# Attention over short sequences: three input buffers, a TensorE loop of twelve steps, and more stores among the loads

## Chip, cores, metric

The kernel runs on one core of one Trainium2 chip. The metric is device time in microseconds (us), lower is better. Times of one kernel on one chip spread by 1 to 3% (the kernel before, 23 runs on one chip: 135.31 to 139.74 us); the state of a run (fast or slow) is given by rule, a run more than 1.5% above the fastest of its kernel counting as slow.

## The reference

For each of 32 x 12 heads, a sequence of 128 and a head dimension of 64, all float32:

```
scores = (1 / sqrt(64)) * q @ k.T
attn   = softmax(scores, axis=-1)
out    = attn @ v
```

This is 37.75 MB to read and 12.58 MB to write for little arithmetic.

## The kernel before

The heads are cut into 48 units of 8 heads. Four units form a group, and a group needs one load each of q, k and v (1 MB read, 0.5 MB written, the tensors being float32 and the buffers bfloat16: the page has 37.75 MB read from HBM for 36 loads and 512.0 KB for each of them). A unit becomes one or two stores. All loads and most stores are issued by GpSimd (POOL) in one program order. TensorE (PE) runs a real loop of `PERIOD` steps. One step holds transposes (T), a reordering of v (V), scores (S) and attention times v (O, Q), each of another unit: T runs five steps ahead of O.

```python
PERIOD, FIRST = 8, -8                        # loop of 8 steps; the first is step -8
TRIPS = NU // PERIOD + 1                     # NU = 48 units
NQ, NVB, NVE, NT, NA = 2, 2, 8, 2, 4         # buffers of q and k, v, reordered v, transposes, attn
MIXED, OWN, HELD = 28, 40, NU - 8            # units stored among the loads
...
# a load waits until its buffer was read by TensorE
if x >= NVB: deps = [("V", sum(vgroups[:x - NVB + 1]) - 1)]                    # v
if x >= NQ:  deps = [("T", t) for t in t_order if t[0] == x - NQ and t[1] == j] # q, k
...
# after the k load of group x: the stores that are due
while kind == "k" and sum(stores[:todo[0] + 1]) <= MIXED * (x - 4) / (len(supers) - 5):
    store(todo.pop(0))
```

The first real work is at step -5, so in the first trip the steps before it have nothing to do, and in the last trip some pieces have nothing to do. Each piece of the loop is therefore under a test of the trip number. Neighbouring pieces that are skipped in the same trip share one test, that is one jump over all of them:

```python
for place in [(l, kind) for l in range(PERIOD) for kind in "TVSOQ"]:
    ...
    skipped = 0 if trips[0] else TRIPS - 1
    if waiting or not places or places[-1][0] != skipped or place == (2, "T"):
        places.append((skipped, waits[place] if waiting else [], []))
    places[-1][2].append((ops[place], [] if waiting else waits[place]))
...
with nc.Fori(0, TRIPS, ..., head_slot={nc.tensor.engine: 144}):   # place of the loop's first
    for skipped, always, some in places:                          # instruction in a block, taken
        run_waits("PE", always)                                   # as 256 from the stops below
        with nc.tensor.If_ne(trip, skipped):
            for o, w in some:
                run("PE", o, w)
    nc.tensor.reg_add(trip, trip, 1)
```

The softmax here doesn't subtract the row's maximum and nothing guards it: scores larger than these inputs give would overflow.

Of the kernel before, what the change touches and what calls it, by code (L numbers as in the profile page):

```python
# [10 lines left out]
def kernel(  # L11
# [7 lines left out]
    nc = tc.nc  # L19
# [12 lines left out]
    NU = B * H // 8  # L32
# [31 lines left out]



    PERIOD, FIRST = 8, -8
    TRIPS = NU // PERIOD + 1


# [7 lines left out]
        v_at[m - 4] = [m]  # L78
    steps = range(min(t_at), NU + 1)

    NQ, NVB, NVE, NT, NA = 2, 2, 8, 2, 4



    MIXED, OWN, HELD = 28, 40, NU - 8

    HALVES = NU - 5

# [360 lines left out]
    def waits_of(engine, o):  # L449
        out = []  # L450
        for name, value in needed(engine, o, c).items():
            have = seen[engine].get(name, 0)
            if value > have:
                out.append((name, value - have if engine == "PE" else value))
                seen[engine][name] = value
        return out

    def run_waits(engine, waits):
        for name, value in waits:
            i = ENGINE[engine].wait_ge(sems[name], value)  # L460
            if engine == "PE":
                i.then_inc(sems[name], -value)
# [3 lines left out]
    def run(engine, o, waits):  # L466
        e = ENGINE[engine]
        run_waits(engine, waits)
        for s, value in o.dma:
            e.wait_ge(s, value)  # L470
        if o.emit is None:

            untold[engine] = o.marks
            return
        i = o.emit()
        for n, name in enumerate(o.marks):
            (i if n == 0 else e.drain()).then_inc(sems[name], 1 + untold[engine].count(name))  # L477
        untold[engine] = []

    def tensor_program():  # L480

        ops, waits, when = {}, {}, {}
        for o in program["PE"]:
            trip, l = divmod(at_step[o.key] - FIRST, PERIOD)
            place = l, o.key[0]
            w = waits_of("PE", o)
            assert waits.setdefault(place, w) == w and not o.dma, (o.key, w, waits[place])
            when.setdefault(place, []).append((trip, o.emit is None))
            if trip == 2:
                ops[place] = o  # L490
        places = []
        for place in [(l, kind) for l in range(PERIOD) for kind in "TVSOQ"]:
            trips = [t for t, empty in when[place] if not empty]
            assert trips in (list(range(TRIPS - 1)), list(range(1, TRIPS))), (place, trips)
            waiting = len(when[place]) > len(trips)
            assert not waiting or len(when[place]) == TRIPS
            skipped = 0 if trips[0] else TRIPS - 1
            if waiting or not places or places[-1][0] != skipped or place == (2, "T"):
                places.append((skipped, waits[place] if waiting else [], []))
            places[-1][2].append((ops[place], [] if waiting else waits[place]))  # L500
        trip = ctx.enter_context(nc.tensor.register("trip"))
        nc.tensor.reg_mov(trip, 0)


        with nc.Fori(
                0, TRIPS, engines=bass.OrderedEngineSet([nc.tensor.engine]),
                head_slot={nc.tensor.engine: 144}):
            for skipped, always, some in places:
                run_waits("PE", always)
                with nc.tensor.If_ne(trip, skipped):  # L510
# [3 lines that stand above are left out]
# [11 lines left out]
    nc.gpsimd.drain()  # L525

    tensor_program()


# [51 lines left out]
```

## Time and profile before

| | before |
|---|---|
| time, median of 3 runs | 136.31 us (135.97 to 136.35) |
| span of the profiled run | 133.8 us |
| busiest compute engine | PE, 70% of the span |
| DMA, mean over the span | 236 GB/s on the written side |
| instruction fetches of TensorE (queue q8) | 4 of 16,384 bytes, at 2.6, 8.3, 15.2 and 20.8 us |

In the rows of 40 slices each slice is a fortieth of that run's span (3.3 us here); digits are busy tenths. In a row of a timeline the first number is the start, the second the busy time, "x16" a count of merged instructions, and the bracket tells how long the engine had stood idle and what ended that. The landing times quoted below come from the trace's completion records: a transfer is counted as landed when the last of the 16 DMA engines that report on it has done so. Fetch times come from its transfer records. That q8 serves TensorE is an inference.

### The profile page before, as it was taken

The page shows a single profiled execution, that of the slowest core. Times are in us where ns is not written, and L with a number is a line of the kernel's source. Part 1 is how long each engine was busy: PE and PEld are TensorE (multiplying, and loading weights), DVE is VectorE, ACT ScalarE, POOL GpSimd, SP SyncE. Part 2 cuts the span into 40 slices and gives each one's busy share as a digit, 9 for nine tenths or more (in the row PEclk, how much of TensorE's full clock was granted, in tenths as well). Part 3 has the DMA queues.
Part 4 walks back from the last instruction along what each step waited for, and adds up shares of the span by engine and source line. Part 5 has one row for each costly group of instructions (what it writes and reads, how often), then busy time and mean ns, then how long its engine had stood idle before and what let it go on. Part 6 is the DMA issues. An engine that isn't in the chain of part 4 may idle for free. (4 is left out here: it accounts for less than half of the span.)

```text
span 133.8 us, 6648 instructions
## 1 busy us (share of the span) xinstructions
PE 93.1 (70%) x2880; PEld 63.3 (47%) x2880; DVE 75.0 (56%) x164; ACT 73.8 (55%) x97; POOL 57.5 (43%) x81
## 2 busy tenths in 40 slices
PE   0052788969869898588657897667897696595820
PEld 0040545636546665365435565445565464464510
DVE  1020346858768775656647458548457547485850
ACT  0005157686758886275573565582656654768700
POOL 5902024060510957705903924914913999500000
PEclk9999999999999999779997579998569869999555
DMA  2999999999999999999999999999999999999971
GB/s 13 162 200 210 200 211 180 194 199 172 212 200 210 188 163 241 309 200 263 314 198 257 319 202 248 327 200 245 331 201 241 331 205 235 390 403 389 359 243 68
DMA packets 24392, 31.56 MB, mean 236 GB/s; under 512 B 1344, under 2 KB 15680, under 8 KB 24384
## 3 DMA queue, kind: packets, MB, share of 16 engines
q0 software_dynamic: 22208, 29.36, 106.7%
q1 hardware_dynamic: 2176, 2.10, 4.6%
q8 instruction: 4, 0.07, 0.2%
q14 instruction: 4, 0.03, 0.1%
HBM read 37.75 MB, written 12.58 MB: 376 GB/s over the span
## 5 line engine op out<-in xcount | busy, mean ns | idle before, releaser
L241 DVE COPY qkT<-qk_ps 128x1024 bf16<-128x1024 bf16 x48 | 33.1, 689 | 34.3 <-DMA k_b<-in_k_dram 19.4
L224 ACT CAST v_e<-v_ps 128x512 bf16<-128x512 f32 x48 | 28.3, 590 | 41.6 <-PE v_ps L186 26.6
L229 ACT ACTIVATE attnT<-s_ps 128x1024 bf16<-128x1024 f32 x48 | 49.5, 1032 | 1.1 <-PE s_ps L205 1.1
L254 DVE TENSOR_TENSOR o_sb<-o_ps,recip 128x512 f32<-128x512 f32 (+1 forms) x53 | 34.0, 642 | 4.8
L383 POOL DMA_DIRECT2D v_b<-in_v_dram x12 | 10.8, 901 | 52.7 <-PE v_ps L186 47.1
L176 PE MATMUL qk_ps<-ident,q_b 128*64 128x128 bf16 x384 | 17.0, 236 | 17.5 <-PEq L460 17.3
L368 POOL DMA_DIRECT2D out_dram<-o_sb x38 | 27.7, 733 | 0.6 <-DVEq L477 0.6
L176 PE MATMUL qk_ps<-ident,k_b 128*64 128x128 bf16 x384 | 18.9, 253 | 12.4 <-PEq L460 12.3
L216 PE MATMUL o_ps<-v_e,attnT 128*32 128x65 bf16 x1536 | 24.1, 205 | 2.2 <-PEq L460 2.0
L176 PEld LDWEIGHTS qk_ps<-ident,q_b 128*64 128x64 bf16 x384 | 13.4, 119 | 20.3 <-issue 19.9
L186 PE MATMUL v_ps<-v_b,sel 128*32 128x512 bf16 x192 | 21.1, 430 | 2.4 <-PEq L460 1.4
L176 PEld LDWEIGHTS qk_ps<-ident,k_b 128*64 128x64 bf16 x384 | 15.2, 131 | 15.5 <-issue 14.5
L216 PEld LDWEIGHTS o_ps<-v_e,attnT 128*32 128x32 bf16 x1536 | 17.8, 101 | 8.7 <-issue 5.2
L205 PE MATMUL s_ps<-qkT 64*128 64x128 bf16 x384 | 20.8, 233 | 0.8 <-PEq L460 0.6
L205 PEld LDWEIGHTS s_ps<-qkT 64*128 64x128 bf16 x384 | 11.8, 100 | 12.7 <-issue 12.7
L251 DVE RECIPROCAL recip<-o_ps 128x8 f32<-128x8 f32 (+1 forms) x53 | 10.5, 199 | 11.8 <-PE o_ps L216 11.3
L395 POOL DMA_DIRECT2D q_b<-in_q_dram x12 | 8.8, 737 | 5.2 <-PE qk_ps L176 4.1
L186 PEld LDWEIGHTS v_ps<-v_b,sel 128*32 128x32 bf16 x192 | 5.1, 94 | 7.9 <-issue 4.7
L395 POOL DMA_DIRECT2D k_b<-in_k_dram x12 | 8.5, 707 | 0.0
L224 ACT ACT_TABLE_LOAD x1 | 1.3, 1283 | 10.8 <-DMA v_b<-in_v_dram 10.8
L539 DVE COPY sel<-ident 128x128 bf16<-128x128 bf16 x1 | 0.2, 227 | 2.2 <-POOL ident L519 2.2
L365 POOL DMA_DIRECT2D out_dram<-o_sb x2 | 1.5, 742 | 0.0
(7 smaller groups left out, 1.1 us busy)
## 6 DMA issues: line engine op xcount, KB each, us to landing
out_dram<-o_sb POOLq DMA_DIRECT2D x40, 256.0 KB, 11.1
q_b<-in_q_dram POOLq DMA_DIRECT2D x12, 512.0 KB, 12.3
v_b<-in_v_dram POOLq DMA_DIRECT2D x12, 512.0 KB, 10.2
k_b<-in_k_dram POOLq DMA_DIRECT2D x12, 512.0 KB, 11.8
out_dram<-o_sb SPq DMA_DIRECT2D x8, 256.0 KB, 5.4
```

The costliest lines, as they stand in the source:

```text
L176: i = nc.tensor.transpose(p[a * D:(a + 1) * D, :, r4, jj, :], x[:, r, a], ident[:])
L186: x = nc.tensor.matmul(t[r4 * 32:(r4 + 1) * 32], lhsT=sel[:, w, :], rhs=v_b[g % NVB][:, :, r4 * D:(r4 + 1) * D], start=True, stop=True)
L205: i = nc.tensor.matmul(t[:, a, h, :], lhsT=x[p, 1, 4 * w + h, :], rhs=x[p, 0, 4 * w + h, :], start=True, stop=True)
L216: y = nc.tensor.matmul(t[h * SO:(h + 1) * SO, a, r * (D + 1):(r + 1) * (D + 1)], lhsT=x[:, a, h, r * SO:(r + 1) * SO], rhs=v_e[m % NVE][:, ...
L224: return nc.scalar.copy(v_e[m % NVE][:, :, :D], v_ps[:].rearrange("p (n e) -> p n e", e=D))
L229: return nc.scalar.activation(out=attnT[u % NA][:].rearrange("p a h (r s j) -> p (a h r) s j", r=4, j=J), in_=s_ps[u % 2][:].rearrange("p ...
L241: return nc.vector.tensor_copy(x.rearrange("p h (r j s) -> p (h r) j s", r=4, j=J)[:, :, 2 * b:2 * b + 2, :].rearrange("p x j s -> p x (j ...
L251: nc.vector.reciprocal(r, o4[:, :, :, D]).then_inc(s_r, 1)
L254: return nc.vector.tensor_mul(o[:, :, w, :].rearrange("p a (r d) -> p a r d", d=D), o4[:, :, :, :D], r.unsqueeze(3).to_broadcast([128, o4. ...
L368: e.dma_start(out=dst[:, a], in_=src[:, a]).then_inc(s_o[lane(c)], 16)
L383: op("POOL", ("load", kind, x), lambda: nc.gpsimd.dma_start(out=v_b[x % NVB][:], in_=v_rows[:, 2 * first:2 * (first + n), :],).then_inc(s_ ...
L395: nc.gpsimd.dma_start(out=bufs[x % NQ][:], in_=rows[R][:, n:n + 2, :]).then_inc(sm[x % NQ], 16)
```

## The change

The intent is to keep a third group of loads in flight, so that the DMA queue does not run thin, and to store more units among the loads. Three buffers repeat every three groups, that is every twelve steps, so the loop must cover twelve steps. The whole diff:

```diff
-    PERIOD, FIRST = 8, -8
+    PERIOD, FIRST = 12, -12
...
-    NQ, NVB, NVE, NT, NA = 2, 2, 8, 2, 4
-    MIXED, OWN, HELD = 28, 40, NU - 8
+    NQ, NVB, NVE, NT, NA = 3, 3, 12, 3, 4
+    MIXED, OWN, HELD = 32, 40, NU - 8
...
-            if waiting or not places or places[-1][0] != skipped or place == (2, "T"):
+            if waiting or not places or places[-1][0] != skipped:
...
-                head_slot={nc.tensor.engine: 144}):
+                head_slot={nc.tensor.engine: 160}):
```

## The prediction

> **What bounds the kernel now.** I read the page first, then throughput by stretch, then GpSimd's timeline (it issues every load), then the end on VectorE and SP. The page's second part:

> ```profile
> DMA  2999999999999999999999999999999999999971
> GB/s 13 162 200 210 200 211 180 194 199 172 212 200 210 188 163 241 309 200 263 314 198 257 319 202 248 327 200 245 331 201 241 331 205 235 390 403 389 359 243 68
> ```

> The DMA row is full from the second slice to the last but two, while no compute engine is above 70% busy on the page: the transfers are the bound. A busy digit does not say that the transfers run at full rate; the GB/s row does. It counts bytes on the written side, and a load writes half of what it reads (float32 becomes bfloat16), so about 205 for loads and about 400 for stores are the same HBM rate. In this light the 180, 172 and 188, 163 are holes. The next view is busy time, clock, DMA share and GB/s in chosen stretches:

> ```profile
> 10.00:21.00 11.00, 7.01 (x132) 4.08 (x131) 2.94 (x5) 5.11 (x8) 2.51 (x4) 1.00 1.21 209
> 21.30:24.00 2.70, 2.33 (x80) 1.75 (x80) 2.10 (x6) 1.98 (x3) 0.21 (x1) 1.00 1.21 162
> ...
> 29.80:32.60 2.80, 2.40 (x80) 1.75 (x80) 2.20 (x6) 1.41 (x2) 0.00 (x0) 1.00 1.21 164
> 32.60:45.40 12.80, 10.98 (x402) 7.58 (x400) 9.42 (x20) 9.69 (x15) 4.20 (x6) 1.00 1.22 207
> 45.40:51.20 5.80, 5.14 (x200) 3.57 (x191) 5.00 (x10) 4.02 (x6) 3.60 (x6) 1.00 1.22 159
> 61.69:102.48 40.79, 31.68 (x970) 21.57 (x972) 24.36 (x49) 24.16 (x32) 20.98 (x29) 0.83 1.19 258
> 114.00:124.00 10.00, 6.93 (x262) 4.62 (x256) 6.34 (x15) 7.73 (x11) 1.68 (x3) 0.96 1.03 394
> 124.00:132.00 8.00, 3.47 (x116) 2.30 (x112) 4.34 (x16) 2.32 (x3) 0.00 (x0) 0.50 0.79 271
> ```

> See the last column: 207 to 209 where loads are well fed, 162, 164 and 159 in three holes, 394 in the stores after the loads, and 271 in the last 8 us. GpSimd's timeline names the cause of the holes:

> ```profile
> 19.21 0.89 POOL L383 DMA_DIRECT2D v_b<-in_v_dram  x1 [7.85 <-PE v_ps L186]
> ...
> 26.62 0.89 POOL L383 DMA_DIRECT2D v_b<-in_v_dram  x1 [5.11 <-PE v_ps L186]
> ...
> 43.51 0.89 POOL L383 DMA_DIRECT2D v_b<-in_v_dram  x1 [6.15 <-PE v_ps L186]
> ```

> GpSimd stands 5 to 8 us before each v load until TensorE has read the v buffer two groups back; the k load and next q load queue behind it in program order. Each of these three issues is followed, 2 to 3 us later, by a hole. The completion records say the same: v loads land 2.6 us after the transfer before them when fed, but 3.51, 3.36 and 3.59 us after it in the three holes, and the k load after the last one 2.99 instead of 2.5. From 55 us on stores lie between the groups, the queue is deeper at each v issue, and v loads land at 2.65 us again: there the two buffers suffice.

> The end is a second, different limit:

> ```profile
> 116.03 0.69 DVE L241 COPY qkT<-qk_ps 128x1024 bf16<-128x1024 bf16 x1 [1.55 <-DMA k_b<-in_k_dram]
> ...
> 128.82 0.42 DVE L254 TENSOR_TENSOR o_sb<-o_ps,recip 128x256 f32<-128x256 f32 x1
> ```

> The last k load lands at 115.9. VectorE is waiting for it, and the seven steps that remain finish at 129.24; SP issues the last store at 129.32 and it lands at 132.29. So 13.4 us of dependent compute plus about 3 us of store follow the last load. The queue drains in parallel, but 271 GB/s in the last 8 us says it is no longer full: compute hands out the last stores.

> [...] a load group alone costs 3 x 524 KB at 207 GB/s = 7.6 us, a stored unit 262 KB at about 400 = 0.65 us, and a group with four units measures 40.79 / 4 = 10.2 us, equal to 7.6 + 4 x 0.65. Moving a store among the loads hides nothing. [...] in the last store: its first engine reports 1.97 us after issue. [...] The page of before shows four 16 KB instruction fetches (q8, 0.07 MB).

> **The change part by part.**

> Third q, k and v buffer. A v load now waits for the group three back, so one more whole group (7.6 us) is queued when it is issued. That is far above the roughly 1 us by which before falls short, so the holes vanish. Their worth from throughput: 2.70 x (1 - 162/207) + 2.80 x (1 - 164/207) + 5.80 x (1 - 159/207) = 0.59 + 0.58 + 1.34 = 2.5 us. From the landings: 0.9 + 0.75 + 0.95 + 0.5 = 3.1 us. I take **2.8 us** earlier for everything after 55 us.

> The third transposed buffer and the twelve v_e buffers remove waits on VectorE and ScalarE that the trace does not show as costs; TensorE's order of steps is unchanged. Worth 0. They are needed because the loop repeats buffer names every three groups, hence twelve steps.

> Stores among the loads. The condition counts units allowed after k load x as 28(x-4)/7, now 32(x-4)/7, cut to whole stores. Before the last k load (x = 11) GpSimd has queued 24 units; now 4, 8, 12, 18, 22, 26. The last k load therefore stands behind two more units: 2 x 0.65 = **1.3 us later**. In exchange 22 rather than 24 units remain after it. Total bytes do not change. I checked that no store should block a load for long: after k loads 8, 9 and 10 the newest stored unit is finished within a step of the k load's own release, with more than a group still queued.

> Loop of twelve steps. Per unit 60 matmuls and 60 weight loads, so 12 x 120 = 1,440 instructions[...]; six fetches instead of four, once. Trip 0 now skips seven steps instead of three while TensorE waits for the first load (its first matmul is at 7.33 us). Any delay there is covered by nine loads in flight. Worth 0, at worst some tenths.

> Sum. Last k load lands at 115.9 - 2.8 + 1.3 = 114.4. Compute path: + 13.4 = 127.8 for the last store's issue, + 2.2 to 3.0 = 130.0 to 130.8 against 132.3, a gain of 1.5 to 2.3. Drain path: 2.8 less work-time lost, 129.5, not the later one. So the extra early stores give back part of what the buffers win. I choose a gain of 2.1 us: 136.3 - 2.1 = **134.2 us**.

> **Rivals.** (a) The drain sets the end and the compute path has slack: then all 2.8 to 3.1 us arrive, 133.2 to 133.5, just over 2% faster. For it: stores on SP land every 0.65 us up to the last, so the slowest DMA engine still had work. Against it: 271 GB/s in the last 8 us. (b) A new wait: GpSimd, with stores closer behind compute, stalls on an unfinished unit and loads fall behind; or [...] issue slows. For it: GpSimd's single program order. Against: a spare group in the queue. It would give 135 to 136. (c) Holes are not starvation but the v loads' 512-byte packets: no gain, only the 1.3 us later, 137.0 to 137.5. Against it: later v loads land at 2.65 us. (d) TensorE's first trip stalls on fetching the longer loop: some us of early compute, caught up before the end. No cost.

> **Range and chances.** Between (a) and the main sum lie 133.2 and 134.8; the range adds a partial (b) and the run spread of 0.4 us: 133.0 to 135.8. The 2% line is 133.58, inside (a): I give faster 0.31, same 0.67, slower 0.02.

> **What would show it.** No stretch below 195 GB/s between 10 and 50 us; GpSimd's v loads issued at least a group earlier; first stores about 2.5 us earlier in the drain; last k landing near 114.4; still 13 us from there to the last normalise; six fetches on q8. I am wrong if holes persist at the same rate, if the last k load lands before 113.5 or after 116, or if the tail after it shortens by over 1 us (the clock there is 0.50, and a livelier clock could do that).

## More of the kernel before

The page's line on instruction fetches:

```profile
q8 instruction: 4, 0.07, 0.2%
```

It gives the count, the megabytes and the share of the DMA engines' time.

## The result

The changed kernel took **146.97 us** (median of 4 runs, 145.13 to 147.5) against 136.33 us. The ratio is 1.0745, with a 95% interval of 1.0616 to 1.0873: slower by 7%. (A ratio here is the mean time of one kernel's fast runs over that of the other's fast runs of the same rounds, so not quite the ratio of the medians.) The prediction was 134.2 us, and wrong.

The page of the changed kernel (slices of 3.6 us), the rows that answer to those of before, and the line of the instruction fetches:

```profile
DMA  2999999999995099949999999999999999999952
GB/s 14 180 206 206 208 207 202 215 199 210 190 212 100 5 129 162 348 95 141 153 347 194 245 320 199 282 348 200 246 319 196 281 282 202 318 401 394 323 177 79
...
q8 instruction: 11, 0.18, 0.5%
```

From the third slice up to slice 12 the throughput is nearly what was predicted: 190 to 215 with hardly a hole. Then it falls to 100, 5 and 129, and again to 95, 141 and 153, where before had 210, 188, 163. After 73 us the row is again like that of before. So nearly everything is lost between 43 and 73 us. The landing times agree: two v loads land 9.60 and 5.39 us after the transfer before them (2.65 when fed), an excess of 6.95 + 2.74 = 9.7 us, and the last store lands 11.2 us later than before (143.45 against 132.29). The predicted two additional stores ahead of the last k load account for up to 1.3 of that.

What starved the DMA is on GpSimd's timeline:

```profile
19.98 0.89 POOL L383 DMA_DIRECT2D v_b<-in_v_dram  x1 [8.76 <-PE v_ps L186]
...
34.35 0.90 POOL L383 DMA_DIRECT2D v_b<-in_v_dram  x1 [12.07 <-PE v_ps L186]
...
49.50 0.89 POOL L383 DMA_DIRECT2D v_b<-in_v_dram  x1 [12.41 <-PE v_ps L186]
...
63.82 0.90 POOL L383 DMA_DIRECT2D v_b<-in_v_dram  x1 [9.10 <-PE v_ps L186]
```

The v loads come 14 to 15 us apart, while a group of loads lasts 7.6 us. GpSimd waits for TensorE to free a buffer. The buffers are not too few; TensorE is slow. TensorE's timeline in that stretch says why:

```profile
22.21 0.46 PE L216 MATMUL o_ps<-v_e,attnT 128*32 128x65 bf16 x17
25.27 0.41 PE L216 MATMUL o_ps<-v_e,attnT 128*32 128x65 bf16 x15 [2.61 <-issue]
25.61 1.06 PE L176 MATMUL qk_ps<-ident,k_b 128*64 128x128 bf16 x16
...
30.34 0.46 PE L216 MATMUL o_ps<-v_e,attnT 128*32 128x65 bf16 x20
32.86 0.28 PE L216 MATMUL o_ps<-v_e,attnT 128*32 128x65 bf16 x12 [2.06 <-issue]
...
37.08 0.52 PE L216 MATMUL o_ps<-v_e,attnT 128*32 128x65 bf16 x23
40.02 0.27 PE L216 MATMUL o_ps<-v_e,attnT 128*32 128x65 bf16 x9 [2.42 <-issue]
...
44.40 0.40 PE L216 MATMUL o_ps<-v_e,attnT 128*32 128x65 bf16 x26
47.34 0.24 PE L216 MATMUL o_ps<-v_e,attnT 128*32 128x65 bf16 x6 [2.54 <-issue]
```

```profile
PE o_ps L216 <- issue: 15.3, 6, 5.5
```

For much of this stretch TensorE is also slow: 16 transposes often take 1.06 us instead of 0.64, and a step up to 2.65 us instead of 1.7. Why is not shown; the granted clock was 0.93 from 22 to 36 us and 0.74 from 36 to 50 us. From one stop to the next, two steps or half a group, 6.8 to 8.1 us pass, which is the 14 to 15 us per group.

The one piece of the diff that I had not read as a change is the removed `place == (2, "T")`. It broke the long jump of the first trip in two. From the ruler the loop's layout is estimated (head at slot 160, six instructions, then 125 a step): in the changed kernel the first trip's jump over seven empty steps leads from block 0 to about slot 160 + 6 + 7 x 125 = 1041, in block 4, over blocks 1, 2 and 3. Before, with three empty steps and the break, it went from block 0 to block 1 (slot 400) and then to block 2 (slot 525).

### The profile page after: what moved, and what is told of

The parts are those of the page before. It is cut to its first block, busy times and chain, and to the rows that moved or that the text cites. A ratio compares the mean times of both kernels' runs of the same rounds, so it can differ in the third digit from the quotient of the medians.

```text
span 145.0 us, 6636 instructions
## 1 busy us (share of the span) xinstructions
PE 99.2 (68%) x2880; PEld 66.7 (46%) x2880; DVE 75.5 (52%) x168; ACT 74.6 (51%) x97; POOL 57.4 (40%) x81
## 2 busy tenths in 40 slices
DMA packets 24399, 31.68 MB, mean 218 GB/s; under 512 B 1344, under 2 KB 15680, under 8 KB 24384
## 5 line engine op out<-in xcount | busy, mean ns | idle before, releaser
L241 DVE COPY qkT<-qk_ps 128x1024 bf16<-128x1024 bf16 x48 | 33.0, 687 | 23.0 <-PE qk_ps L176 11.0
L216 PE MATMUL o_ps<-v_e,attnT 128*32 128x65 bf16 x1536 | 25.7, 209 | 16.6 <-issue 15.3
L254 DVE TENSOR_TENSOR o_sb<-o_ps,recip 128x512 f32<-128x512 f32 (+1 forms) x53 | 34.0, 642 | 4.8
L383 POOL DMA_DIRECT2D v_b<-in_v_dram x12 | 10.9, 907 | 55.8 <-PE v_ps L186 47.7
L176 PE MATMUL qk_ps<-ident,q_b 128*64 128x128 bf16 x384 | 21.2, 274 | 16.2 <-PEq L460 15.8
L216 PEld LDWEIGHTS o_ps<-v_e,attnT 128*32 128x32 bf16 x1536 | 18.3, 104 | 24.2 <-issue 21.0
L251 DVE RECIPROCAL recip<-o_ps 128x8 f32<-128x8 f32 (+1 forms) x53 | 10.6, 201 | 34.0 <-PE o_ps L216 33.1
L176 PEld LDWEIGHTS qk_ps<-ident,q_b 128*64 128x64 bf16 x384 | 16.8, 144 | 19.1 <-issue 18.3
L186 PE MATMUL v_ps<-v_b,sel 128*32 128x512 bf16 x192 | 22.6, 460 | 1.8 <-PEq L460 1.0
L205 PE MATMUL s_ps<-qkT 64*128 64x128 bf16 x384 | 22.2, 245 | 0.7 <-PEq L460 0.6
L176 PE MATMUL qk_ps<-ident,k_b 128*64 128x128 bf16 x384 | 17.8, 243 | 4.9 <-PEq L460 4.1
L205 PEld LDWEIGHTS s_ps<-qkT 64*128 64x128 bf16 x384 | 12.6, 104 | 14.0 <-issue 14.0
L176 PEld LDWEIGHTS qk_ps<-ident,k_b 128*64 128x64 bf16 x384 | 14.0, 124 | 7.8 <-issue 6.7
L186 PEld LDWEIGHTS v_ps<-v_b,sel 128*32 128x32 bf16 x192 | 5.1, 95 | 7.6 <-issue 4.7
```

Of the source, the lines that this page charges most:

```text
L176: i = nc.tensor.transpose(p[a * D:(a + 1) * D, :, r4, jj, :], x[:, r, a], ident[:])
L186: x = nc.tensor.matmul(t[r4 * 32:(r4 + 1) * 32], lhsT=sel[:, w, :], rhs=v_b[g % NVB][:, :, r4 * D:(r4 + 1) * D], start=True, stop=True)
L205: i = nc.tensor.matmul(t[:, a, h, :], lhsT=x[p, 1, 4 * w + h, :], rhs=x[p, 0, 4 * w + h, :], start=True, stop=True)
L216: y = nc.tensor.matmul(t[h * SO:(h + 1) * SO, a, r * (D + 1):(r + 1) * (D + 1)], lhsT=x[:, a, h, r * SO:(r + 1) * SO], rhs=v_e[m % NVE][:, ...
L241: return nc.vector.tensor_copy(x.rearrange("p h (r j s) -> p (h r) j s", r=4, j=J)[:, :, 2 * b:2 * b + 2, :].rearrange("p x j s -> p x (j ...
L251: nc.vector.reciprocal(r, o4[:, :, :, D]).then_inc(s_r, 1)
```

## The experiments

**Theory "skipped blocks"**: the long jump leaves blocks of the loop unfetched, and the next pass has to fetch block after block on demand, behind the queued loads. **Rivals**: the 32 units among the loads hold up GpSimd ("stores behind compute"); nine loads in flight slow the issue or the transfers ("queue depth"); a loop of seven blocks is too long by itself ("loop too long").

### First set: repair it, or undo one part

**e1_split.** Two breaks, so that the first trip's jumps are short:

```diff
-            if waiting or not places or places[-1][0] != skipped:
+            if waiting or not places or places[-1][0] != skipped or place in ((2, "T"), (4, "T")):
```

> The changed kernel, but TensorE's first trip passes the seven empty steps in three short jumps (about 240 instructions each) instead of one of about 840, so that it touches each 256-instruction block. Theory 'skipped blocks' (the one long jump leaves two blocks of the loop unfetched, and the next pass fetches block after block on demand): TensorE's 2 to 5.5 us stalls between 22 and 62 us vanish, about 7 instruction fetches instead of 11, time 133 to 136 us. Theories 'stores behind compute', 'queue depth' and 'a loop of seven blocks is too long': no change, 145 to 148 us.

Measured: 135.21 us median of 20 runs (133.62 to 136.51) against 136.97; ratio 0.9839 (0.9801 to 0.9876), 1.6% faster than before. Six fetches. One condition in the building of the loop is worth 9% of the time. All three rivals fall: stores, buffers and the loop's length are those of the slow kernel. Two stops, of 2.88 and 1.98 us, remain; they end at 19.3 and 24.8 us. The first matmul is at 12.9 us instead of 7.2.

**e2_first5.** `FIRST = -5`: the first trip has work in each step, and no jump passes a block.

```diff
-    PERIOD, FIRST = 12, -12
+    PERIOD, FIRST = 12, -5
```

> The changed kernel with the loop's first step at -5 instead of -12: the first trip has work in every step and jumps over single pieces only. The loop has the same length. 'Skipped blocks': no long stalls, 6 or 7 fetches, 133 to 136 us. 'Loop too long': fetch stalls remain at the same places of the loop, 143 us or more. 'Stores' and 'queue depth': unchanged, 145 to 148 us.

Measured: 139.83 us against 136.97, ratio 1.0231 (1.0126 to 1.0335), and six fetches. Of the ten surplus us about three are left: fetches at 32.3 and 39.9 us come with stops of 4.48 and 1.93 us. So the theory is too narrow. In this run blocks that are reached for the first time late, when nine loads stand in the queue and TensorE has work, go with these stops even though nothing was skipped; to that extent the rival "loop too long" has a share. (The profiled run was slow; the stops are read for their presence only.)

**e3_mixed28.** 28 units among the loads as before.

```diff
-    MIXED, OWN, HELD = 32, 40, NU - 8
+    MIXED, OWN, HELD = 28, 40, NU - 8
```

> The changed kernel with 28 units among the loads as before. 'Stores behind compute': the loss goes, 135 to 137 us. 'Skipped blocks' and the others: the stalls are in TensorE before most stores, so 144.5 to 147 us, at most 1.3 us better.

Measured: 145.89 us, ratio 1.0683 (1.0589 to 1.0778), eleven fetches (the profiled run was a slow one). The stores are not the cause.

**e4_depth2.** Three buffers, but loads wait for the group two back.

```diff
-            if x >= NVB:
-                deps = [("V", sum(vgroups[:x - NVB + 1]) - 1)]
+            if x >= 2:
+                deps = [("V", sum(vgroups[:x - 1]) - 1)]
...
-        if x >= NQ:
-            deps = [("T", t) for t in t_order if t[0] == x - NQ and t[1] == j]
+        if x >= 2:
+            deps = [("T", t) for t in t_order if t[0] == x - 2 and t[1] == j]
```

> The changed kernel with three buffers, but each load still waits for the group two back, so no more loads are in flight than before. 'Queue depth' (nine loads in flight slow the issue or the transfers): back to 136 to 138 us. 'Skipped blocks': the same TensorE stalls with less prefetched data behind them, 147 to 155 us.

Measured: 153.72 us, ratio 1.1263 (1.1151 to 1.1376), eleven fetches. The depth is no cause; by the two ratios it softened the stops by some 7 us.

### Second set: the same fault in the old kernel, and where the blocks lie

**e5_before_nosplit.** The kernel *before*, with its break removed and nothing else:

```diff
-            if waiting or not places or places[-1][0] != skipped or place == (2, "T"):
+            if waiting or not places or places[-1][0] != skipped:
```

> The kernel before with one thing of the change alone: the extra break in the loop's skipped part is taken out, so that the first trip passes its three empty steps in one jump of about 375 instructions, out of the block with the loop's head and over the next one (head at slot 144, a step is about 125 instructions, so the jump ends near slot 525 of blocks of 256). Loads, buffers and stores are those of before. 'Skipped blocks': more than 4 instruction fetches, TensorE stalls of 2 us or more in the first full pass, and since only 4 to 5 us of loads are queued here, 139 to 147 us. Rival 'only the longer loop or the third buffers make it slow': as before, within 1% of 136.5 us.

Measured: 149.28 us against 136.64, ratio 1.0921 (1.0854 to 1.0989). Nine fetches instead of four. TensorE's timeline:

```profile
22.15 0.57 PE L216 MATMUL o_ps<-v_e,attnT 128*32 128x65 bf16 x25
24.66 0.24 PE L216 MATMUL o_ps<-v_e,attnT 128*32 128x65 bf16 x7 [1.95 <-issue]
...
28.78 0.58 PE L216 MATMUL o_ps<-v_e,attnT 128*32 128x65 bf16 x28
32.51 0.21 PE L216 MATMUL o_ps<-v_e,attnT 128*32 128x65 bf16 x4 [3.15 <-issue]
```

The same stops, again three matmuls further after two steps, and eight matmuls, that is 16 instructions, later than in the changed kernel (after 25 and 28, not 17 and 20), as the head of the loop lies 16 slots earlier; this in a kernel with the old buffers, stores and loop length. A third stop, of 4.12 us, is in step 6. The 9.2% are due to the removed break alone; this is the cleanest proof. The old kernel's odd-looking condition keeps this loss away, whether or not it was meant to.

**e6_split3.** Breaks before steps 2, 4 and 6, because with two breaks the last jump still passes block 3 (slot 666 to 1041).

```diff
+            ... or place in ((2, "T"), (4, "T"), (6, "T")):
```

> The changed kernel with breaks before steps 2, 4 and 6 of the loop, so that no jump passes over a whole block (with the two breaks of the run before, the last jump still passed one: from slot 666 to about 1041). 'Skipped blocks': no stall over 1.5 us after the first matmul, the third v group's load issued earlier than 26.7 us, 133.5 to 135.5 us. If the demand fetches at the start merely move (each break is one more fetch behind the loads), the first matmul is later than 12.9 us and the time equals that with two breaks, 134.5 to 136.

Measured: 138.9 us, ratio 1.0163 (1.0101 to 1.0226): not better but worse than with two. Its first matmul and that of e1_split:

```profile
17.69 1.06 PE L176 MATMUL qk_ps<-ident,q_b 128*64 128x128 bf16 x16 [17.69 <-PEq L460]
```

```profile
12.86 1.06 PE L176 MATMUL qk_ps<-ident,q_b 128*64 128x128 bf16 x16 [12.86 <-PEq L460]
```

Fetches are at 2.9, 8.7, 15.0 and 20.6 us. They come 5.6 to 6.3 us apart, one after another, the first three before TensorE's first matmul. With two breaks the loads queued by then, which last to 31.6 us in e12_split2_again below, cover the late start; with three the next v load is issued at 30.85 us, and lands 5.99 us after the transfer before it. Of the second alternative the late first matmul came, but not its time of 134.5 to 136 us. Two stops, of 2.03 and 2.09 us, also remain after the first matmul, where none over 1.5 us was expected.

**e9_head0.** Head at slot 0, so that by the ruler the loop lies in six blocks, and breaks before steps 3 and 5.

```diff
+            ... or place in ((3, "T"), (5, "T")):
...
-                head_slot={nc.tensor.engine: 160}):
+                head_slot={nc.tensor.engine: 0}):
```

> The changed kernel with the loop's head at slot 0 of a block instead of 160, so that it lies in six blocks instead of seven, and breaks before steps 3 and 5, so that no jump passes a whole block. 'Skipped blocks': no stall over 1.5 us after the first matmul, one fetch fewer, 133 to 135.5 us. If the place of the head does not matter, the same as with the three breaks.

Measured: 140.47 us, ratio 1.0251 (1.0175 to 1.0328); still six fetches, first matmul at 16.7 us, and stops of 2.63 and 2.23 us. A miss: a block fewer saved nothing, as here, by the layout, two touched blocks cost nearly what three did in e6_split3.

### Third set: the prediction's own steps, on the repaired kernel, and what makes a fetch slow

**e12_split2_again.** e1_split unchanged, for comparison on the same chip.

> The kernel with the two breaks once more, unchanged, so that it stands on the same chip as its two variants: again 1 to 2% faster than before, 134 to 135.5 us.

Measured: 133.65 us (133.44 to 135.54) against 136.66, ratio 0.9789 (0.9734 to 0.9843). The lowest median, and it beats both kernels. Over the two sets it is 1.6 and 2.1% faster than before.

**e10_split2_mixed28.** The same with 28 units among the loads (the edit of e3_mixed28).

> The changed kernel with the two breaks that repaired it, and 28 units among the loads. The prediction's step 'two more units ahead of the last k load make the end 1.3 us later': 1 to 1.5 us faster than the same kernel with 32. Rival 'the end is set by the drain of all bytes': the same within 0.4 us.

Measured: 135.15 us, ratio 0.9831 (0.9758 to 0.9903). The intervals overlap: the expected gain of 1 to 1.5 us with 28 did not come, and no difference is shown. In the profiled runs the last k load landed at 114.32 us with 28 and at 114.16 with 32. Without the two stores it should have come 1.3 us earlier; but that run had thin stretches of its own between 27 and 40 us (189, 179, 195, 173 GB/s, where e12_split2_again has 208, 200, 212, 200). With 28 the last store landed 4.35 us after issue, with 32 it took 2.53. In these two profiles, then, the drain seems to set the end with more stores left over, and the compute chain with fewer; one profile of each does not show it.

**e11_split2_depth2.** The repaired kernel with loads gated two groups back (the edits of e1_split and e4_depth2).

> The changed kernel with the two breaks, each load waiting for the group two back, as before. The prediction's step 'the third group in flight fills the holes and is worth 2.8 us': 2.5 to 4 us slower than with three, more if the late first matmul (near 12.9 us) is no longer covered by queued loads, 138 to 142 us. If the depth is worth nothing: the same.

Measured: 143.88 us, ratio 1.0456 (1.0386 to 1.0526), so some 9 us slower than with depth three, more than expected. Its GB/s row has 48 and 13 at 21 to 28 us: the late first matmul is no longer covered. The third group in flight is needed to pay for the longer loop's start; what it is worth beyond that this run cannot separate.

**e13_split3_gated.** e6_split3, but the loads of groups 1 and 2 wait for TensorE's first two transpose steps. Slow on purpose.

```diff
-        deps = []
+        deps = [("T", (0, 0, 1))] if 0 < x < NVB else []
```

> The kernel with three breaks, but loads of the second and third group are held back until TensorE has done its first two transpose steps, so that only three loads are ahead of its instruction fetches and the DMA queue is empty from about 13 us. It is slow on purpose. If a fetch is slow because it shares the DMA engines with queued loads: the fetches at the start, 5.6 to 6.3 us apart with nine loads queued, come within 1.5 to 3 us of each other once the three loads are done, and the first matmul is at 11 to 14 us instead of 17.7. If a fetch takes 5.6 us by itself: the same spacing and 17.7.

Measured (one look): fetches at 2.5, 8.2, 11.6, 14.8 and 18.1 us. The first two, with three loads in the queue, are 5.8 us apart; the third comes 3.4 us later, when the last of the three loads is about to land (12.9 us), and the others, with none in the queue, 3.2 and 3.3 us after the one before. First matmul at 14.4 instead of 17.7. In this one run part of the slowness, some 2.4 of 5.8 us per fetch, goes with the loads ahead of it. The expected 1.5 to 3 us was missed: over 3 us remain without any loads.

### Last: undo that part of the change alone

**e14_keep_break.** The change with the old condition left in.

```diff
-            if waiting or not places or places[-1][0] != skipped:
+            if waiting or not places or places[-1][0] != skipped or place == (2, "T"):
```

> The change with one of its parts undone: the old break before step 2 of the loop is kept. The jumps then end in block 1 (slot about 416) and block 4 (about 1041); blocks 2 and 3 are still passed over, where the change as it stands passes 1, 2 and 3. 'Skipped blocks', each passed block being paid for in the next pass: fetches between 6 and 11, fewer or shorter stalls than in the change, first matmul before 12 us, 137 to 145 us. If the break does nothing by itself: 145 to 148 us with 11 fetches. If one break is enough: 133.5 to 135.5.

Measured: 141.65 us (138.81 to 142.92) against 138.02, ratio of the fast runs 1.0346 (1.0253 to 1.0439); two of its five runs were fast. Ten fetches, the tenth at 108.8 us, long after the loop's first passes. TensorE's first stops:

```profile
32.32 0.33 PE L216 MATMUL o_ps<-v_e,attnT 128*32 128x65 bf16 x10 [2.72 <-issue]
...
39.76 0.30 PE L216 MATMUL o_ps<-v_e,attnT 128*32 128x65 bf16 x7 [2.67 <-issue]
```

The first begins at 29.6 us, in step 4, not at 22.7 in step 0; three more follow in steps 6, 8 and 10. The time lies between the unrepaired kernel and the repaired one, as the theory has it. The detail does not fit it: by the ruler the stops are the entries into blocks 3 to 6. Block 2, which the jump passed, has no stop, and blocks 4 to 6, which the first trip had run through, have one each. The changed kernel stops at the entries into 4 and 6 too. So the long jump is what costs, but "each passed block is paid for" is not the rule.

The groups of runs in order, each against the kernel before on its own chip:

| kernel | blocks passed over in the first trip | fetches | first matmul, us | ratio to before |
|---|---|---|---|---|
| before | none | 4 | 7.3 | 1 |
| e5: before, no break | 1 | 9 | 7.5 | 1.092 |
| changed | 1, 2, 3 | 11 | 7.2 | 1.0745 |
| e14: one break | 2, 3 | 10 | 9.5 | 1.035 |
| e1, e12: two breaks | 3 | 6 | 12.9 | 0.984, 0.979 |
| e6: three breaks | none | 6 | 17.7 | 1.016 |

The passed blocks are worked out from the layout; the trace does not say which block a fetch brings. The ratio does not follow the count of passed blocks alone: e6 passes none and is slower than e1 and e12, which pass one and start earlier.

## Why the prediction was wrong

**The bound, and the holes.** Right in e12_split2_again, in part in e1_split. In e12_split2_again the v loads that had left holes land 2.62 to 2.68 us after the transfer before them, and the stretch from 10 to 50 us reads, in the kernel before, in e12_split2_again and in e1_split:

```profile
10.00:50.00 40.00, 31.42 (x992) 21.02 (x989) 24.67 (x49) 26.83 (x36) 12.85 (x17) 1.00 1.21 195
```

```profile
10.00:50.00 40.00, 30.38 (x855) 20.40 (x855) 22.01 (x42) 23.00 (x31) 12.54 (x17) 1.00 1.23 206
```

```profile
10.00:50.00 40.00, 29.84 (x848) 20.07 (x850) 21.80 (x42) 22.74 (x30) 12.29 (x17) 1.00 1.22 200
```

The last column is GB/s. e1_split is the same kernel, profiled in a fast run, and still has four slices of 187 to 191, below the 195 that the prediction allowed. Rival (c), that the holes are due to small packets, is out.

**The sum.** Its terms for the loads hold in one of the two profiles of the repaired kernel. Predicted: last k load at 114.4 us, last store landed at 130.0 to 130.8, time 134.2. In the profiled run of e12_split2_again: 114.16 us, 130.08 us, and 133.65 us as the median. In that of e1_split: 116.08 us, which is no earlier than before, 132.15 us, and 135.21 us as the median. So the close agreement of the first is partly luck; what is shown is the gain in time over both sets, 1.6 and 2.1% where 1.5% was predicted.

**The stores.** The term of 1.3 us is not confirmed by time (e10_split2_mixed28). The prediction set the compute path as the later of the two ends by about 0.5 to 1.3 us; the profiles of e10_split2_mixed28 and e12_split2_again suggest that the ends are so close that moving two units only changes which one it is.

**The loop of twelve steps.** This is the step that failed. The prediction said "six fetches instead of four, once" and "Any delay there is covered by nine loads in flight. Worth 0, at worst some tenths." In its place the runs showed eleven fetches, six stops of 15.3 us in total, a slowed TensorE between them, and v loads that land 9.7 us late in sum: 10.6 us lost in the median, and all six stops in the second trip. Three things went wrong in it. I counted the instructions of the loop, which gives a number of fetches and not what the first pass costs; it was only the later passes that were free of them (after 64.2 us there is no further fetch). I took the first trip's skip as free because TensorE waits for the first load anyway, while the cost falls in the *second* trip. And I passed over the removed break. Rival (d) named the fetch stall and put it at no cost; nine loads are 23 us of cover, but TensorE at 14 to 15 us per group against 7.6 us of loads uses that up in three groups.

**Rival (b)**, GpSimd held by unfinished stores: not seen as a cause, since e3_mixed28 stays slow with fewer stores, and so does e4_depth2 with fewer loads in flight.

**What stays open.** Why blocks that the first trip had run through are fetched again after the long jump (eleven fetches for seven blocks; stops at the entries into blocks 4 to 6 in e14_keep_break). Whether the few instructions of the break itself, which shift all later code, matter apart from where the jumps land. Whether fetching goes ahead of need, and how far (the fetch at 49.8 us came 2.5 us before its stop of 0.20 us). What makes a fetch take 3.2 us with an empty queue, when the transfer of the 16,384 bytes takes 0.89 to 0.97 us in the kernel before and 0.89 to 1.46 us in the changed one; and why in e12_split2_again, with loads queued, two fetches come 0.9 us apart, against 5.6 to 6.3 us in e6_split3. Whether 28 or 32 is better by less than 1%.

## What to carry to other kernels

The loop here had no fetch after 64.2 us, yet its first full pass cost 15.3 us of stops: look where the jumps of such a loop land in blocks as the stops measure them (256 instructions here), and count the fetches on the instruction queue against the number of blocks (11 against seven). When an engine stops in the middle of equal instructions with nothing to wait for, note after how many; if the place moves by a constant from one time to the next, suspect a block boundary, and look for a fetch at each stop. And a condition in the code that has no visible reason is part of a change that removes it: undo it alone.
